# From attention to the output projection of layer 0: a relay of divisors on another queue, a reciprocal in four pieces, and two tiles that take the last heads last

## The chip, the cores and the metric

The kernel is one program for one NeuronCore of a Trainium2 chip. That core has five engines that run at the same time, each with its own list of instructions in a fixed order: TensorE (PE in the profile, with its weight loads as PEld), VectorE (DVE), ScalarE (ACT), GpSimd (POOL) and SyncE (SP). An engine that waits for a semaphore holds back everything that stands behind it in its own list. Data moves by DMAs, which are issued by SP and POOL here and carried out by 16 DMA engines that all queues share.

The metric is device time in microseconds (us) of one execution, and the median over several runs is what counts. Matrix products run in fp32 precision by splitting each operand into a rounded high part and a remainder, so that one product takes three matmuls: high·high, high·low and low·high.

## The reference, cut to what matters

The model has two layers over 1024 positions with a width of 1024. Layer 0 is the one touched here: 12 heads of causal attention with 64 value columns each, beside 4 memory heads, joined and sent through one output projection.

```python
def causal_dense_attention(q, k, v):            # blocks of 128 queries, cut
    sc = einsum('bqhd,bkhd->bhqk', q_blk, k) * scale
    sc = where(mask, sc, NEG)
    p = softmax(sc, axis=-1)
    return einsum('bhqk,bkhd->bqhd', p, v)

for i in range(DEPTH):
    hn = rmsnorm(x, attn_norm_g[i])
    mix, q_cross = mla_mixer(hn, ...) if i % 2 == 0 else swa_mixer(hn, ...)
    cross = memory_cross_attention(q_cross, mem_n, w_mem_kv[i])
    x = x + concatenate([mix, cross], axis=-1) @ w_o[i]
    x = x + squared_relu_mlp(rmsnorm(x, mlp_norm_g[i]), w_up, w_down)
return rmsnorm(x, final_norm_g)
```

The softmax is computed without its division first: the sum of the weights of each query, the divisor, comes out of the same matmul as the weighted values, and the head's output is multiplied by its reciprocal afterwards.

## The kernel before

**Attention.** The loop over `seq` goes through heads 0 to 11, and for each through 12 blocks `(G, k)`: G is one half of the queries (512 columns), k one tile of 128 keys. `scores` (L913) makes the scores of a block in a PSUM tile `pss` by three matmuls; DVE adds the mask on the diagonal part (L921); ACT takes the exponential into `p` (L923). For G = 1 the weights stay whole. For G = 0 they are split (L99 on ACT, L100 on DVE) into `ph` and `pl`. `values` (L943) multiplies them by the values into `pso`, one PSUM tile per head and half. Rows 0 to 63 of `pso` are the head's output, rows 64 to 127 its divisor.

**The heads' divisors.** The outputs of heads 0 to 10 are copied out (L969) and sent by SP to their place in `qn` (L970, called `fa` in the profile for the tiles of heads 8 to 11), and their divisors to a small tile `den` (L973). The heads are divided in groups: 0 to 5, 6 to 9, and 10 alone. For a group, `rc_split` takes the reciprocals of its divisors (L1000), POOL writes them to DRAM (L1001, `rcd`), and POOL reads them back, spread over 64 partitions (L993, `rb`), in two halves of the queries. `rc_mul` (L1010) then multiplies the outputs in place on DVE. For head 10 these are `rb_0_1` (second half) and `rb_0_0` (first half). Head 11 goes another way: `last_o` takes the reciprocal of all 512 columns straight from PSUM (L980) and multiplies (L981), the second half at the end of its values, the first half only inside the output projection.

**The output projection.** `wo_phase` goes over the output columns in two halves. The first half uses weights `wq` loaded earlier (`woq` in the profile); the weights `w1` of the second half are loaded by SP (L689) and split (into `g`) while the first half runs. In the first half the eight row tiles are taken in the order 4, 5, 6, 7, 0, 1, 2, 3, so position p = 0 is tile 4. For each, `load` fetches the tile of x (SP, L1203, two positions ahead); `osp` splits the heads' outputs into high and low parts (`x` in the profile, L99 on ACT and L100 on DVE); `mm3` adds up eight terms in PSUM (`pswo`), 24 matmuls of 512 columns (L108, L109, L110); and DVE adds x (L1278). ACT then takes the sum of squares (L1144). The terms are numbered by pairs of heads: 0 to 3 are heads 0 to 7, 4 is heads 8 and 9, 5 is heads 10 and 11, 6 and 7 are the memory heads. The order is 0, 1, 2, 3, 6, 7, 4, 5. For tiles 4 and 5 the split of terms 4 to 7 goes in two pieces, the memory heads first.

**What sets the order.** The program is recorded in the order of the text, and a scheduler then places the instructions on each engine, mostly by when their operands are due, so the lists of ACT and DVE mix work from attention and projection. DMAs of one engine stand in that engine's list too, so SP issues the loads of x only after what stands ahead of them.

Of the kernel before, what the change touches and what calls it, by code (L numbers as in the profile page):

```python
# [14 lines left out]
ALU = mybir.AluOpType  # L15
# [4 lines left out]
P = 128  # L20
# [35 lines left out]
def trunk(  # L56
# [7 lines left out]
    nc = tc.nc  # L64
    x = x[0]
    out = out[0]
# [518 lines left out]
    halves = [slice(0, 512), slice(512, 1024)]  # L585
# [209 lines left out]
    qn = [(f0, f1)[j // 4][:, j % 4, :] for j in range(6)]  # L795
# [8 lines left out]
    for j in range(6):  # L804
# [4 lines left out]
        ps = ps2(f"pskn{j}")  # L809
# [164 lines left out]

        return mms, then

    def last_o(G, tmp):

        po = po_[(H - 1, G)]
        nc.vector.reciprocal(tmp, po[64:128])  # L980
        nc.vector.tensor_tensor(qn[5][64:128, G * 512 : (G + 1) * 512], po[0:64], tmp, ALU.mult)  # L981


    GRP = [0, 6, 10, 11]
# [4 lines left out]
    def rc_pair(c, j, i):  # L989

        rb = at.tile([P, 512], F32, tag="rb", bufs=4, name=f"rb{c}_{j}_{i}")
        for e in range(min(2, GRP[c + 1] - GRP[c] - 2 * j)):
            nc.gpsimd.dma_start(out=rb[e * 64 : e * 64 + 64, :], in_=rc_d[c][2 * j + e, halves[i]].partition_broadcast(64))  # L993
        return rb

    def rc_split(c):

        n = (GRP[c + 1] - GRP[c]) * NT
        rc = at.tile([48, P], F32, tag="rc", bufs=1, name=f"rc{c}")[:n]
        nc.vector.reciprocal(rc, den[c])  # L1000
        nc.gpsimd.dma_start(out=rc_d[c].rearrange("h (t p) -> (h t) p", p=P), in_=rc)  # L1001
        r_tiles[c] = [(j, i) for j in range((GRP[c + 1] - GRP[c] + 1) // 2) for i in (1, 0)]
        r_tiles[c] = [(j, i, rc_pair(c, j, i)) for j, i in r_tiles[c]]

# [16 lines left out]
    LV, LB = 3, 5  # L1021
    NB = len(blocks)
# [12 lines left out]
    for n in range(len(seq) + LB):  # L1035
        ms, mv, then = [], [], []
        if n < len(seq):
            ms, then_s = scores(*seq[n])
        for lag, late in ((LB, True), (LV, False)):
            if 0 <= n - lag < len(seq):  # L1040
                a, b = values(*seq[n - lag], late)
                mv += a
                then.append(b)

        mix = []
        if ms and mv and P in [width(*seq[n - lag][1:]) for lag in (0, LV, LB)]:
            while ms and mv:
                mix += [ms.pop(0), mv.pop(0)]
        for f in mix + ms:
            f()  # L1050
        if n < len(seq):
            then_s()
        for g, i in ahead.get(n, ()):
            if i < NT:
                row_max(g, i)
            else:
                max_row(g)
        h, j = divmod(n, NB)
        if n < len(seq):
            if h + 1 < H and j == 6:  # L1060
                v_tiles(h + 1)
            if h + 1 < H and j == 8:
                v_full(h + 1)
            if j == (0 if h else 4) and h + 2 < H:
                head_tiles(h + 2)
        for f in mv:
            f()
        for f in then:
            f()
        if n % 2 or n > 11 * NB:  # L1070
            next(muls, None)
        if n >= 9 * NB + 8 and n % 3 == 0:
            wq.step()
        for c in range(3):
            if n == GRP[c + 1] * NB + LB + 1:
                rc_split(c)
            if n == GRP[c + 1] * NB + LB + (8 if c == 2 else 11):
                muls = rc_mul(c)
    for _ in muls:
        pass  # L1080
# [75 lines left out]
    def wo_phase(layer, wq, o, m):  # L1156
# [10 lines left out]
        def o_split(t, parts_=(0, 1), x=None):  # L1167

            r = []
            for i in parts_:  # L1170
                if x is None and layer == 1 and oct_[0] == 0:
                    d = ores.tile([P, 2, 512], F32R, name="ores0")
                    oct_[0] += 1
                elif x is None:
                    d = m.t(f"d{oct_[0] % 3}", F32R)
                    oct_[0] += 1
                else:
                    if x not in ox:
                        ox[x] = m.t(f"x{x % 4}", F32R)
                    d = ox[x][:, 2 * i : 2 * i + 2, :]  # L1180
                oh, ol = k4(d[:, 0, :]), k4(d[:, 1, :])
                src = o[i][:, :, t * P : (t + 1) * P]
                for ks in (slice(2, 4), slice(0, 2)) if i and x in (0, 1) else (slice(0, 4),):
                    split(src[:, ks, :], oh[:, ks, :], ol[:, ks, :])
                r += [(oh[:, k, :], ol[:, k, :]) for k in range(4)]
            return r
# [63 lines left out]
        for half, w in enumerate((wq, w1)):  # L1250
            order = ORD[half]

            def osp(p, parts_):
                t = order[p]
                if half == 1 and t in kept:
                    return kept[t][4 * parts_[0] : 4 * parts_[-1] + 4]
                r = o_split(t, parts_, p if layer == 0 and half == 0 else None)
                if half == 0 and layer == 0 and p in (5, 7):
                    kept[t] = kept.get(t, []) + r
                return r  # L1260

            xs = {0: load(0, half), 1: load(1, half)}
            oo = {0: osp(0, (0, 1))}
            for p in range(NT):
                t = order[p]
                if p + 2 < NT:
                    xs[p + 2] = load(p + 2, half)
                ps = ps1(f"pswo{layer}_{half}_{t}")
                ot = oo.pop(p)
                if p + 1 < NT:  # L1270
                    oo[p + 1] = osp(p + 1, (0,))
                mm3(ps, [(*ot[k], *w.w[k]) for k in (0, 1, 2, 3, 6, 7, 4, 5)])
                if p + 1 < NT:
                    oo[p + 1] += osp(p + 1, (1,))
                if p == 1 and layer == 0 and half == 0:
                    last_o(0, m.t("i39")[0:64, 0, :])
                x_ = xs.pop(p)
                nc.vector.tensor_tensor(x_, ps, x_, ALU.add)  # L1278
                if half == 0:
                    w1.step()  # L1280
                    rst[t] = Rstd()
                    rst[t].half(0, x_, m.t(f"d{3 + p % 2}")[:, 0, :])
                    continue
                for i, v_ in enumerate((xa[t], x_)):
                    nc.gpsimd.dma_start(out=xd[rows_(t), i * 512 : i * 512 + 512], in_=v_)
                norm(p, x_)
                if p:
                    xT_(p - 1)
                if p in (2, 4):
                    m.fill.append(fill_w(layer, m, p // 2 - 1))  # L1290
            if half == 0:
                if layer == 0:
                    new_psum(2)
                for i in range(2):
                    q = m.quad(f"q{i}", F32R)
                    X[i + 1] = [q[:, 0:4, :], q[:, 4:8, :]]
# [781 lines left out]
```

## Time and profile before

| | |
|---|---|
| Median of 3 runs | 2145.2 us (2143.55 to 2147.43) |
| Profiled execution, first to last instruction (span) | 2151.4 us |
| PE busy | 2113.6 us, 98% of the span |
| DVE busy | 1473.3 us, 68% |
| ACT busy | 1106.6 us, 51% |
| POOL busy | 148.9 us, 7% |
| Mean granted TensorE clock | 0.994 |

The profiled execution's own time is given by its span alone: first to last instruction takes 2151.4 us, and what lies around that is not shown. This is 6.2 us, or 0.3%, more than the median of the timed runs.

How to read the rows: a row of the timeline gives the start in us from the span's start, the time from the start of the first to the end of the last instruction in that row, the engine, the line of the kernel, the operation, what it writes and reads, and the shape. Behind it, in brackets, stands how long the engine had been idle before it and what it was waiting for. A row by stretches of time gives, for each engine, the busy time and the number of instructions; then the granted TensorE clock (1.00 is full speed) and the DMA engines' busy share and rate. Matmuls overlap each other, so the time of one is longer than the step from one start to the next.

### The profile page before, as it was taken

The numbers are of one execution on the slowest core, as the hardware profiler recorded it, in microseconds if no ns is written. First come the engines' busy times: TensorE is split into PE (matmuls) and PEld (weight loads), VectorE is DVE, ScalarE is ACT, GpSimd is POOL, SyncE is SP. The second block draws the span as 40 slices with busy tenths as digits, with TensorE's granted clock in tenths as the row PEclk, the third lists the DMA queues.
The fourth block names the chain that finished last, engine by engine and source line by source line (L and its number), as shares of the span: only waits on it lengthen the run. The fifth ranks groups of instructions, "written<-read, shape, count | busy, mean of one in ns | idle before, by whom it ended". The sixth has DMA issues, their size and how long they took to land.

```text
span 2151.4 us, 28963 instructions
## 1 busy us (share of the span) xinstructions
PE 2113.6 (98%) x9830; PEld 1697.7 (79%) x9830; DVE 1473.3 (68%) x2915; ACT 1106.6 (51%) x2406; POOL 148.9 (7%) x251
## 2 busy tenths in 40 slices
PE   7999999989999999999999999999999999999998
PEld 6888766668888788888888878668888888788886
DVE  7767677764987677886557632776987766876665
ACT  6555466655754543444445432866844453444453
POOL 1001001010000000000001121530000000000000
PEclk9999999999999999999999999999999999999999
DMA  6202223333354445954433534132354446954432
GB/s 225 84 1 71 54 67 92 94 114 103 103 174 144 138 162 190 326 179 147 146 115 108 152 79 118 40 128 84 103 181 142 140 149 212 321 167 142 133 119 87
DMA packets 176436, 286.84 MB, mean 133 GB/s; under 512 B 16627, under 2 KB 68448, under 8 KB 176288
## 3 DMA queue, kind: packets, MB, share of 16 engines
q1 hardware_dynamic: 169648, 266.30, 39.1%
q0 software_dynamic: 5328, 16.07, 2.1%
q10 hardware_dynamic: 1312, 2.63, 0.4%
q8 instruction: 77, 1.26, 0.2%
q14 instruction: 71, 0.58, 0.1%
HBM read 183.01 MB, written 76.85 MB: 121 GB/s over the span
## 4 chain that ended last, share of the span: by engine, by line
PE 90%; DVE 4%; DMA 3%; ACT 2%; issue 1%; POOL 0%; SPq 0%; DVEq 0%; ACTq 0%; POOLq 0%
PE psy L1705 5%; PE psy L1707 5%; PE psy L1706 5%; PE psu L1402 5%; PE psu L1404 5%; PE psu L1403 5%; PE psz L1705 4%; PE psz L1707 4%; PE psz L1706 4%; PE psv L1404 4%; PE psv L1403 4%; PE psv L1402 4%; PE pso L943 3%; PE pss L913 3%; PE pswo L110 3%; PE pswo L108 3%
## 5 line engine op out<-in xcount | busy, mean ns | idle before, releaser
L1302 ACT ACTIVATE mr<-mr,gcol 128x256 f32<-128x256 f32 (+1 forms) x160 | 67.6, 477 | 79.4 <-DMA mr<-in_mlp_w_up_dram 70.4
L923 ACT ACTIVATE p<-pss 128x512 f32<-128x512 f32 (+2 forms) x144 | 68.4, 486 | 69.3 <-DVE pss L921 52.4
L1705 PE MATMUL psy<-g 128*128 128x512 f32 x256 | 99.9, 390 | 0.0
L1706 PE MATMUL psy<-g 128*128 128x512 f32 x256 | 99.6, 389 | 0.0
L1707 PE MATMUL psy<-g 128*128 128x512 f32 x256 | 99.4, 390 | 0.0
L99 ACT ACTIVATE g<-i 128x512 fp32r<-128x512 f32 x79 | 49.7, 629 | 93.5 <-PE psz L1706 46.3
L1302 ACT ACTIVATE d<-d,gcol 128x256 f32<-128x256 f32 x128 | 57.6, 500 | 75.2 <-DMA d<-in_mlp_w_up_dram 61.4
L100 DVE TENSOR_TENSOR g<-i,g 128x512 fp32r<-128x512 f32 x79 | 55.5, 703 | 47.8 <-ACT g L99 47.8
L99 ACT ACTIVATE i<-mr 128x512 fp32r<-128x512 f32 x78 | 49.1, 630 | 73.7 <-PE psy L1706 26.1
L943 PE MATMUL pso<-p,vf 128*128 128x512 f32 (+2 forms) x192 | 85.4, 527 | 0.5 <-ACT p L923 0.5
L792 DVE TENSOR_REDUCE m<-psx 128x1 f32<-128x1024 f32 (+7 forms) x96 | 71.9, 752 | 20.0 <-PE psx L791 19.6
L99 ACT ACTIVATE uh<-i 128x512 fp32r<-128x512 f32 x66 | 41.7, 631 | 84.6 <-PE psy L1706 39.3
L100 DVE TENSOR_TENSOR uh<-i,uh 128x512 fp32r<-128x512 f32 x66 | 45.5, 689 | 46.2 <-ACT uh L99 46.2
L1705 PE MATMUL psz<-g 128*128 128x512 f32 x192 | 74.7, 389 | 0.0
L1706 PE MATMUL psz<-g 128*128 128x512 f32 x192 | 74.7, 389 | 0.0
L1707 PE MATMUL psz<-g 128*128 128x512 f32 x192 | 74.7, 389 | 0.0
L100 DVE TENSOR_TENSOR i<-mr,i 128x512 fp32r<-128x512 f32 x78 | 53.5, 686 | 21.5 <-ACT i L99 21.5
L913 PE MATMUL pss<-qh,kh 97*128 97x512 f32 (+2 forms) x144 | 68.0, 474 | 0.0
L1618 DVE TENSOR_TENSOR mqf<-mqq,mqf 128x512 f32<-128x512 f32 x64 | 43.3, 686 | 22.1 <-DMA mqq<-in_mlp_w_down_dram 21.9
L913 PE MATMUL pss<-ql,kh 97*128 97x512 f32 (+2 forms) x144 | 58.2, 404 | 0.0
L1707 PEld LDWEIGHTS psy<-g 128*128 128x128 f32 x256 | 48.1, 188 | 10.1
L1706 PEld LDWEIGHTS psy<-g 128*128 128x128 f32 x256 | 48.1, 188 | 9.9
(655 smaller groups left out, 6890.5 us busy)
## 6 DMA issues: line engine op xcount, KB each, us to landing
i<-hd SPq DMA_DIRECT2D x154, 256.0 KB
hd<-uh SPq DMA_DIRECT2D x76, 256.0 KB
hd<-ul SPq DMA_DIRECT2D x76, 256.0 KB
mr<-in_mlp_w_up_dram SPq DMA_DIRECT2D x36, 512.0 KB
hd<-x SPq DMA_DIRECT2D x72, 256.0 KB
mr<-hd SPq DMA_DIRECT2D x70, 256.0 KB
d<-in_mlp_w_up_dram SPq DMA_DIRECT2D x32, 512.0 KB
mqq<-in_mlp_w_down_dram SPq DMA_DIRECT2D x32, 512.0 KB
```

The source lines that it names most:

```text
L99: nc.scalar.activation(hi, src, AF.Copy)
L100: nc.vector.tensor_tensor(lo, src, f32(hi), ALU.subtract)
L792: nc.vector.reduce_max(m8s[h][:, i : i + 1], ps[:, :n], axis=AX, negate=True)
L913: return lambda: nc.tensor.matmul(o, a, b, skip_group_check=True, **kw)
L943: mms.append(lambda: nc.tensor.matmul(o, a, b, skip_group_check=True, **kw))
L1302: nc.scalar.activation(w[:, k, :], w[:, k, :], AF.Copy, scale=g_mlp[layer][:, k0 + k : k0 + k + 1])
L1402: nc.tensor.matmul(ps, wh[:, k, :], xh[:, k, :], start=p in (1, 2, 5) and k == 0, stop=False, skip_group_check=True)
L1403: nc.tensor.matmul(ps, wh[:, k, :], xl[:, k, :], start=False, stop=False, skip_group_check=True)
L1404: nc.tensor.matmul(ps, wl[:, k, :], xh[:, k, :], start=False, stop=k == 3, skip_group_check=True)
L1705: nc.tensor.matmul(ps, ah[:, j, :], bh, start=p in (1, 5, 2) and k == 0, stop=False, skip_group_check=True)
L1706: nc.tensor.matmul(ps, ah[:, j, :], bl, start=False, stop=False, skip_group_check=True)
L1707: nc.tensor.matmul(ps, al[:, j, :], bh, start=False, stop=k == NP - 1, skip_group_check=True)
```

## The change

The change has five parts, all between the end of attention and the first tiles of the output projection of layer 0.

1. For group 2 (head 10 alone) the write of the reciprocals and the two reads are issued by SP instead of POOL. They stand on SP right after head 10's last output, ahead of the loads of x.
2. The point in the text at which head 10's multiplications begin is two steps later (10 instead of 8).
3. `last_o` works in pieces of 128 columns: four reciprocals and four multiplications, each pair in turn. For the second half of the queries all four come at the end of head 11's values. For the first half one piece comes at each of the positions p = 0 to 3.
4. For tiles 4 and 5 the split of terms 4 to 7 goes in three pieces: memory heads, then heads 8 and 9, then heads 10 and 11.
5. Tiles 4 and 5 first run seven of their eight terms each; term 5 (heads 10 and 11) of tile 4 and of tile 5 follows then, and with it the addition of x and the sum of squares of both.

In the resulting lists SP has three more DMAs, standing between `den<-on` and the first `i<-in_x_dram`, and POOL three fewer. DVE has 14 more instructions: six more reciprocals, six more multiplications, two more splits. ACT has two more splits. PE has the same instructions in another order. Before, PE's list has the first two matmuls each of tiles 4, 5 and 6, then the matmul of `pl_0_1`, then the first two of tile 7, then the last four matmuls of head 11, then the rest of tile 4. After, `pl_0_1` comes first, then the first two matmuls of tiles 4 and 5, the last four matmuls of head 11, the first two of tiles 6 and 7, then the rest. On DVE the order of head 10's multiplications, the splits `pl` and the reciprocals is also different: both multiplications stand ahead of `pl_0_1` and `pl_0_2`, with the mask of the block (0, 2) between them, and the reciprocals of head 11 stand behind all of these. Beyond the first half of the projection, the lists differ by a few exchanged neighbours only.

```diff
-    def last_o(G, tmp):
+    def last_o(G, tmp, js=range(4)):
         po = po_[(H - 1, G)]
-        nc.vector.reciprocal(tmp, po[64:128])
-        nc.vector.tensor_tensor(qn[5][64:128, G * 512 : (G + 1) * 512], po[0:64], tmp, ALU.mult)
+        for j in js:
+            c = slice(j * P, (j + 1) * P)
+            nc.vector.reciprocal(tmp[:, c], po[64:128, c])
+            nc.vector.tensor_tensor(qn[5][64:128, G * 512 + j * P : G * 512 + (j + 1) * P], po[0:64, c], tmp[:, c], ALU.mult)
...
-            nc.gpsimd.dma_start(out=rb[e * 64 : e * 64 + 64, :], in_=rc_d[c][2 * j + e, halves[i]].partition_broadcast(64))
+            (nc.sync if c == 2 else nc.gpsimd).dma_start(out=rb[e * 64 : e * 64 + 64, :], in_=rc_d[c][2 * j + e, halves[i]].partition_broadcast(64))
...
-        nc.gpsimd.dma_start(out=rc_d[c].rearrange("h (t p) -> (h t) p", p=P), in_=rc)
+        (nc.sync if c == 2 else nc.gpsimd).dma_start(out=rc_d[c].rearrange("h (t p) -> (h t) p", p=P), in_=rc)
...
-            if n == GRP[c + 1] * NB + LB + (8 if c == 2 else 11):
+            if n == GRP[c + 1] * NB + LB + (10 if c == 2 else 11):
...
-                for ks in (slice(2, 4), slice(0, 2)) if i and x in (0, 1) else (slice(0, 4),):
+                for ks in (slice(2, 4), slice(0, 1), slice(1, 2)) if i and x in (0, 1) else (slice(0, 4),):
...
-            oo = {0: osp(0, (0, 1))}
+            oo, rest = {0: osp(0, (0, 1))}, []
...
-                mm3(ps, [(*ot[k], *w.w[k]) for k in (0, 1, 2, 3, 6, 7, 4, 5)])
+                terms = [(*ot[k], *w.w[k]) for k in (0, 1, 2, 3, 6, 7, 4, 5)]
+                early = layer == 0 and half == 0 and p < 2
+                mm3(ps, terms[: 7 if early else 8], last=not early)
...
-                if p == 1 and layer == 0 and half == 0:
-                    last_o(0, m.t("i39")[0:64, 0, :])
-                x_ = xs.pop(p)
-                nc.vector.tensor_tensor(x_, ps, x_, ALU.add)
+                if layer == 0 and half == 0 and p < 4:
+                    if p == 0:
+                        od = m.t("i39")[0:64, 0, :]
+                    last_o(0, od, [p])
+                rest.append((p, t, ps, terms[7:] if early else None))
+                if early and p == 0:
+                    continue
+                for q, t, ps, term in rest:
+                    if term:
+                        mm3(ps, term, first=False)
+                    x_ = xs.pop(q)
+                    nc.vector.tensor_tensor(x_, ps, x_, ALU.add)
+                    if half == 0:
+                        w1.step()
+                        rst[t] = Rstd()
+                        rst[t].half(0, x_, m.t(f"d{3 + q % 2}")[:, 0, :])
+                rest = []
                 if half == 0:
-                    w1.step()
-                    rst[t] = Rstd()
-                    rst[t].half(0, x_, m.t(f"d{3 + p % 2}")[:, 0, :])
                     continue
```

## The prediction

> **What bounds the kernel now.** I read the page's summary and its chain of waits first, to see which engine a saving must come from; then stretches of time around the change; then the timelines of PE, DVE, POOL and SP in that stretch, to follow the one long stall back to its cause.
>
> ```profile
> span 2151.4 us, 28963 instructions
> PE 2113.6 (98%) x9830; PEld 1697.7 (79%) x9830; DVE 1473.3 (68%) x2915; ACT 1106.6 (51%) x2406; POOL 148.9 (7%) x251
> PE 90%; DVE 4%; DMA 3%; ACT 2%; issue 1%; POOL 0%; SPq 0%; DVEq 0%; ACTq 0%; POOLq 0%
> ```
>
> PE is 90% of the chain that ends last. A microsecond in which PE is idle or slow is paid in full; one saved on another engine counts only if PE waited for it.
>
> ```profile
> 453.00:456.00 3.00, 2.77 (x11) 1.38 (x9) 0.00 (x0) 2.62 (x6) 0.88 (x2) 1.00 0.79 262
> 456.00:461.50 5.50, 0.01 (x1) 0.01 (x1) 4.52 (x4) 0.00 (x0) 0.00 (x0) 0.75 0.02 4
> 461.50:464.50 3.00, 2.55 (x7) 1.57 (x8) 2.94 (x8) 1.93 (x6) 0.00 (x0) 0.50 0.00 0
> 464.50:469.00 4.50, 4.50 (x13) 3.53 (x13) 4.47 (x8) 3.13 (x5) 0.00 (x0) 0.50 0.17 62
> 469.00:477.10 8.10, 8.10 (x36) 6.53 (x35) 6.16 (x8) 2.52 (x6) 0.57 (x1) 1.00 0.09 33
> 477.10:509.50 32.40, 32.40 (x140) 26.07 (x139) 16.00 (x21) 19.59 (x46) 3.24 (x6) 1.00 0.46 146
> ```
>
> After the length stand PE, PEld, DVE, ACT and POOL; the third number from the end is the granted clock. PE does nothing from 456 to 461.5, and then works at a clock of 0.50 until 469. So the stall is paid twice.
>
> ```profile
> 455.49 0.40 PE L109 MATMUL pswo<-woq,x 128*128 128x512 f32 x1
> 461.49 0.69 PE L943 MATMUL pso<-pl,vh 128*128 128x384 f32 x1 [5.60 <-DVE pl L100]
> 464.53 0.73 PE L110 MATMUL pswo<-woq,x 128*128 128x512 f32 x1
> 476.66 0.63 PE L110 MATMUL pswo<-woq,x 128*128 128x512 f32 x2
> 481.79 0.63 PE L110 MATMUL pswo<-woq,x 128*128 128x512 f32 x2
> ```
>
> PE waits for `pl_0_1`, a split of 0.5 us on DVE. The rest of tile 4 begins at 464.53. The pair at 476.66 is tile 5's last matmul and tile 6's first one of the rest, the latter 0.23 later, at 476.89.
>
> ```profile
> 445.34 0.94 DVE L1000 RECIPROCAL rc<-den 8x128 f32<-8x128 f32 x1
> 451.13 0.60 DVE L921 TENSOR_TENSOR pss<-pss,dmaskT 128x128 f32<-128x128 f32 x2
> 456.95 0.68 DVE L1010 TENSOR_TENSOR fa<-rb,fa 64x512 f32<-64x512 f32 x1 [5.22 <-DMA rb<-rcd]
> 457.66 3.36 DVE L980 RECIPROCAL rq<-pso 64x512 f32<-64x512 f32 x1
> 460.94 0.82 DVE L100 TENSOR_TENSOR pl<-p,ph 128x384 fp32r<-128x384 f32 x2
> 461.79 0.69 DVE L981 TENSOR_TENSOR fa<-pso,rq 64x512 f32<-64x512 f32 x1
> 463.32 0.68 DVE L100 TENSOR_TENSOR x<-qn,x 128x512 fp32r<-128x512 f32 x1
> 463.93 0.28 DVE L100 TENSOR_TENSOR pl<-p,ph 128x128 fp32r<-128x128 f32 x1
> 464.13 0.74 DVE L100 TENSOR_TENSOR x<-fa,x 128x256 fp32r<-128x256 f32 x2
> ```
>
> DVE itself waits: `fa<-rb` stands ahead of the splits and needs the divisors of head 10. Behind it come a reciprocal of 3.36 us and only then `pl`.
>
> ```profile
> 432.44 0.50 POOL L1001 DMA_DIRECT2D rcd<-rc  x1 [62.18 <-DVE pl L100]
> 434.37 4.11 POOL L993 DMA_DIRECT2D rb<-rcd  x8 [1.43 <-DMA rcd<-rc]
> 446.57 0.53 POOL L1001 DMA_DIRECT2D rcd<-rc  x1 [8.09 <-DVE rc L1000]
> 452.83 1.05 POOL L993 DMA_DIRECT2D rb<-rcd  x2 [5.73 <-DMA rcd<-rc]
> 443.50 0.61 SPq L973 DMA_DIRECT2D den<-on  x1
> 444.17 8.91 SPq L1203 DMA_DIRECT2D i<-in_x_dram  x10
> ```
>
> The relay through DRAM starts at 446.57, when SP has already issued several of x's loads of 256 KB.
>
> ```profile
> rcd<-rc POOLq DMA_DIRECT2D x1, 16.0 KB, 1.6
> rcd<-rc POOLq DMA_DIRECT2D x1, 4.0 KB, 6.0
> DMA to landing us min/median/max: 2.8/2.9/4.1
> L1000 DVE RECIPROCAL rc<-den x3: 930/934/940, 360.4 to 445.3; 48x128 f32<-48x128 f32 x1, 32x128 f32<-32x128 f32 x1, 8x128 f32<-8x128 f32 x1
> ```
>
> The last number of the first two rows is the time from issue to landing: 1.6 us for the group before, 6.0 for the smaller write of head 10. The third row is that of `rb` (L993). From the end of the reciprocal, 445.34 + 0.94 = 446.28, to `fa<-rb` at 456.95 the relay takes 10.67 us.
>
> **The change part by part.**
>
> *The relay on SP.* POOL started 0.29 after the reciprocal's end (446.57 against 446.28); I keep this for SP. No row gives the landing of such a write from SP. The nearest is `den<-on`, issued at 443.50 and used by DVE at 445.34, so at most 1.84; the write from POOL without x's loads took 434.37 − 432.44 = 1.93 until the next issue. I take 1.93, as this row holds issue, landing and wake-up. For the read I take the shortest of L993's row, 2.8, since no load of x is in flight then. So `rb_0_1` lands at 446.28 + 0.29 + 1.93 + 2.8 = 451.3. DVE is then just done with the first of the two masks (451.13 plus half of 0.60, 451.4), so an earlier landing gains nothing; that is the one end. The other is 10.67 us again, landing at 456.9. `rb_0_0` is issued 0.6 later and lands while DVE works on the first.
>
> A rule speaks against this part. The Trainium skill, "DMA: Bandwidth & Descriptors", section "Issuing engines are not separate DMA queues", says that transfers of all issuing engines share the same 16 DMA engines and interleave, so that another issuing engine saves issue time only. By that alone the relay stays at 10.67 us, and the sum is that of rival B. The two write rows differ by 4.4 us on the same queue, so what stands beside the transfer matters; the order ahead of x removes this whichever engine issues.
>
> *The order on DVE.* From 451.4 on: `fa<-rb_0_1` 0.61 (the step from 463.32 to 463.93), mask 0.2, `fa<-rb_0_0` 0.61, `pl_0_1` and `pl_0_2` 0.82 (the row at 460.94), then for tile 4 three reciprocals of 128 columns with two multiplications, a mask and `pl_0_3`, then the split `x<-qn`. A reciprocal of 128 columns took 0.93 to 0.94 whatever its rows (L1000), a 128-column step 0.20 (463.93 to 464.13). So 0.61 + 0.2 + 0.61 + 0.82 + 3 × 0.93 + 4 × 0.20 + 0.61 = 6.4, and `x<-qn` ends at 457.8. PE follows about 0.1 later, at 457.9, with the rest of tile 4, against 464.53: **6.6 us**.
>
> The four pieces cost 4 × 0.93 = 3.7 instead of 3.36 per half, but the fourth and the later multiplications lie behind `x<-qn`: PE needs `x<-fa` of tile 4 only ten matmuls later, at 457.9 + 10 × 0.233 = 460.2, and DVE has it after 0.93 + 0.2 + 0.4, at 459.4.
>
> *PE until then.* `pl_0_1` comes at 453.7, so PE's work goes on: it has six matmuls of 512 columns, the rest of head 11 and two more, with waits of some tenths for ACT. I count about 1.2 us of idle time in pieces from 453.5 to 457.9. The new wait is that mask (0, 2), hence `ph_0_2`, stands behind `rb_0_1`. It is due on PE at 453.4, and is done at 453.1: 0.3 us of cover. Each us that the relay is later than that stops PE for as long.
>
> *The clock.* Tiles 4 and 5 have 44 matmuls left. Before, they took 464.53 to 476.89, 12.36 us. A tile's 22 take 481.79 − 476.66 = 5.13 at full clock, so 10.26. If the clock stays at 1.00, **2.1 us** more are saved. Rows for both outcomes:
>
> ```profile
> 35.52:38.94 3.42, 1.46 (x6) 0.86 (x5) 3.13 (x11) 1.78 (x4) 0.00 (x0) 1.00 0.00 0
> 38.94:45.76 6.82, 5.54 (x24) 5.17 (x25) 5.74 (x25) 3.52 (x7) 0.00 (x0) 0.50 0.46 155
> 144.75:148.16 3.41, 2.49 (x19) 2.31 (x18) 3.11 (x10) 2.50 (x7) 1.43 (x4) 1.00 0.01 2
> 148.16:151.58 3.42, 3.42 (x25) 3.38 (x24) 2.02 (x4) 3.41 (x12) 0.81 (x1) 1.00 0.00 0
> ```
>
> With 1.46 of 3.42 us busy (43%) the clock fell to 0.50 afterwards; with 2.49 of 3.41 (73%) it did not. I expect about 3.2 of 4.4 busy, 73%.
>
> *The last heads last.* PE does the same 44 matmuls, so it costs nothing there. Tile 4's addition comes after tile 5, and its split buffer is free for the fifth tile 5.1 us later. Cover: tiles 6 and 7, 2 × 5.13 = 10.3 us of PE work, against some 2 us for the splits. Without it, PE would wait those 2 us. The six extra reciprocals and multiplications and two splits on DVE, and two splits on ACT, lie in stretches where these have slack (16.00 and 19.59 busy of 32.40).
>
> *SP and POOL.* SP issues x's first load after both reads, at 446.57 + 1.93 + 1.2 = 449.7 instead of 444.17. It is used at 457.9 + 10.3 = 468.2, so 18 us are left; ten loads took 8.91 to issue before. Everything behind them on SP (the weights of the second half) waits for DVE's and PE's work, which is earlier now. On POOL nothing stood behind the two reads before the first store of x. Cost: nothing. The later start in the text of head 10's multiplications has only the effect of the order above.
>
> *Sum.* 6.6 + 2.1 = 8.7 us. The profiled span goes from 2151.4 to 2142.7. It is 6.2 above the median of 2145.2; I carry the difference over: **2136.5 us**.
>
> **The rivals.**
>
> *A: the clock falls all the same.* If PE's idle pieces meet in one stretch, or the relay is 1 to 2 us later, the share comes down towards 43%. Before, 0.50 lasted from about 458.8 to 469, some 10.2 us (0.75 is the mean of 456 to 461.5); in the rows above, 6.8. With PE at work throughout this costs 3.4 to 5.1: 2139.9 to 2141.6. For it: the margin is thin. Against it: the row at 73%. The Trainium skill, "TensorE: Matmul & The Clock Gate", section "What's actually happening", has the clock halved after one idle window of about 3.4 us; by that rule pieces of idle time of a few tenths leave it alone. The rows above agree at 73%, while at 43% the window was not idle and the clock fell.
>
> *B: the relay takes 10.67 us on SP as well.* Then everything from 451.4 moves by 5.5: PE stops at 453.4, the rest of tile 4 starts at 463.4, and the clock falls as before (about 2.6 lost), so tile 6 begins at 463.4 + 10.3 + 2.6 = 476.3 instead of 476.9: 2144.6, no change. Against it: 1.6 against 6.0.
>
> *C: slower.* The place is DVE's wait for `rb_0_1`: the mask, both `pl` and with them PE now stand behind it, and the six early matmuls too, which before ran during the wait. Past a landing at 457.5 each us costs one; 0.2% slower needs 461.8, a relay of 15.5 us: 2149.5 or more. No row shows one over 10.67.
>
> *D: the gain is given back* in the second half of the projection, if its weights or x come late: 2143 to 2145. Against it: PE is busy 32.40 of 32.40 us up to 509.5.
>
> **How the numbers follow.** Forecast 72%, A 13%, B 6%, D 5%, C 4%. The likeliest one's own range is 2134.3 to 2138.7: the runs lie up to 2.2 from their median, and a read of 4.1 instead of 2.8 gives 1.3. With A it reaches to 2141.6. About 0.2%, 4.3 us, is what a measurement can tell from no change, so faster means below 2140.9: the forecast, half of A and some of D, 83%. Within it lie the rest of A, B and D, 12%; slower 5%, C and what I don't see.
>
> **What would show it.** `rcd` on SP lands in about 2 us and `fa<-rb` starts near 451.4 with next to no wait; PE's 5.60 at `pl` is gone, no idle piece is over 1 us between 453 and 458; tile 4's rest starts near 458; the clock reads 1.00 from 440 to 509; the first addition of x comes near 468 and waits for PE, not for x. The prediction is wrong if `fa<-rb` waits past 453, if the clock reads 0.50 anywhere there, or if an idle piece as long as the gain turns up after 468.

## The result, and the profile after

The changed kernel takes **2139.24 us** (median of 9 runs, 2137.54 to 2141.73), beside 2145.2 us of the kernel before (median of 9 runs, 2142.95 to 2149.52): a ratio of 0.9969, with a 95% interval of 0.996 to 0.9978, or 6.0 us less. Forecast was 2136.5, with 2134.3 to 2141.6 as the range; the likeliest case had 2134.3 to 2138.7 of it, so the measured time lies 0.5 us beyond that part, in what rival A added.

The profiled execution has a span of 2137.4 us, and its own run took 2139.06. From the page of the changed kernel, the same three lines as shown of before:

```profile
span 2137.4 us, 28982 instructions
PE 2107.2 (99%) x9830; PEld 1695.1 (79%) x9830; DVE 1475.4 (69%) x2929; ACT 1106.3 (52%) x2408; POOL 147.3 (7%) x248
PE 92%; DVE 3%; DMA 2%; ACT 2%; issue 1%; SPq 0%; DVEq 0%; ACTq 0%
```

Two spans can't simply be subtracted: 14.0 us lie between these two, and not all of them come from the change. Head 10's reciprocal, which is ahead of all that was edited, ends at 442.06 + 0.94 = 443.00 now and ended at 446.28 before, so 3.3 of the 14.0 are there by then. I therefore count everything from that end, and call a time so counted R+. The first matmul of the projection's second half comes at R+55.06, and came at R+63.28: **8.2 us** around the change. The last 2.5 us are small pieces further back; part of them, near 700 to 880 us, also differs by up to 2 us between two executions of the changed kernel.

The stretch around the change, in the view by stretches of time (length; busy time and number on PE, PEld, DVE, ACT, POOL; granted clock; DMA share and rate):

```profile
449.00:452.00 3.00, 2.71 (x15) 1.87 (x14) 2.91 (x6) 2.70 (x8) 0.00 (x0) 1.00 0.88 278
452.00:455.30 3.30, 2.22 (x10) 1.25 (x9) 3.18 (x7) 2.30 (x8) 0.00 (x0) 1.00 1.02 381
455.30:465.54 10.24, 10.24 (x46) 8.31 (x46) 9.93 (x20) 5.35 (x8) 0.00 (x0) 1.00 0.09 35
465.54:473.80 8.26, 8.26 (x37) 6.72 (x36) 8.07 (x13) 5.74 (x13) 1.66 (x3) 1.00 0.36 134
473.80:506.20 32.40, 32.40 (x142) 26.40 (x141) 14.13 (x20) 18.67 (x44) 3.23 (x6) 1.00 0.41 133
```

The clock is 1.00 in every row. There is no row in which PE does nothing, and DVE is nearly full until 473.8; in the kernel before it stood still for 5.22 us ahead of `fa<-rb`. PE's own rows:

```profile
451.55 0.50 PE L108 MATMUL pswo<-woq,x 128*128 128x512 f32 x1 [0.29 <-ACT x L99]
452.98 0.33 PE L943 MATMUL pso<-ph,vh 128*128 128x128 f32 x1 [0.71 <-ACT ph L99]
453.21 0.43 PE L943 MATMUL pso<-pl,vh 128*128 128x256 f32 x2
454.01 0.50 PE L108 MATMUL pswo<-woq,x 128*128 128x512 f32 x1 [0.37 <-ACT x L99]
455.31 0.40 PE L110 MATMUL pswo<-woq,x 128*128 128x512 f32 x1
465.30 0.62 PE L110 MATMUL pswo<-woq,x 128*128 128x512 f32 x2
```

The wait of 5.60 us for `pl` is gone, and three waits of 0.29, 0.71 and 0.37 us are left. The rest of tile 4 starts at 455.31 (R+12.3, before R+18.25). The pair at 465.30 is the last matmul of tile 5 and the first of tile 6's rest, at 465.53 (R+22.5, before R+30.6). DVE and SP:

```profile
442.06 0.94 DVE L1002 RECIPROCAL rc<-den 8x128 f32<-8x128 f32 x1
447.86 0.29 DVE L921 TENSOR_TENSOR pss<-pss,dmaskT 128x128 f32<-128x128 f32 x1
448.06 0.67 DVE L1012 TENSOR_TENSOR fa<-rb,fa 64x512 f32<-64x512 f32 x1
449.46 0.95 DVE L100 TENSOR_TENSOR pl<-p,ph 128x384 fp32r<-128x384 f32 x2
450.44 0.96 DVE L982 RECIPROCAL rq<-pso 64x128 f32<-64x128 f32 x1
451.43 0.30 DVE L921 TENSOR_TENSOR pss<-pss,dmaskT 128x128 f32<-128x128 f32 x1
451.76 0.28 DVE L983 TENSOR_TENSOR fa<-pso,rq 64x128 f32<-64x128 f32 x1
452.08 0.96 DVE L982 RECIPROCAL rq<-pso 64x128 f32<-64x128 f32 x1
453.60 0.96 DVE L982 RECIPROCAL rq<-pso 64x128 f32<-64x128 f32 x1
454.48 0.62 DVE L100 TENSOR_TENSOR x<-qn,x 128x512 fp32r<-128x512 f32 x1
456.33 0.36 DVE L100 TENSOR_TENSOR x<-fa,x 128x256 fp32r<-128x256 f32 x1
464.93 1.16 DVE L100 TENSOR_TENSOR g<-wor,g 128x1024 fp32r<-128x1024 f32 x1
466.12 1.29 DVE L1290 TENSOR_TENSOR i<-pswo,i 128x512 f32<-128x512 f32 x2
```

```profile
443.03 0.32 SPq L1003 DMA_DIRECT2D rcd<-rc  x1
444.41 1.13 SPq L995 DMA_DIRECT2D rb<-rcd  x2
445.59 8.14 SPq L1205 DMA_DIRECT2D i<-in_x_dram  x11
```

SP issues the write at R+0.03 and the first read at R+1.40. DVE comes to `fa<-rb` at R+5.05, straight from the mask and without a wait, and ends `x<-qn` at 455.10, R+12.1. PE follows 0.2 later, when it has done the four early matmuls of tiles 6 and 7 (454.01 to 455.31).

From the start of `fa<-rb` to the end of `x<-qn` DVE takes 12.10 − 5.05 = 7.05 us. In the kernel before it is the same: 456.95 to 463.32 + 0.68 = 464.00, also 7.05. So DVE's new order and its pieces, taken together, don't bring the split nearer; what is saved up to there is the relay's 10.67 − 5.05 = 5.62.

### The profile page after: what moved, and what is told of

Its sections match the earlier page's. It is cut to its first block, busy times and chain, and to the rows that moved or that the text cites. A ratio compares the mean times of both kernels' runs of the same rounds, so it can differ in the third digit from the quotient of the medians.

```text
span 2137.4 us, 28982 instructions
## 1 busy us (share of the span) xinstructions
PE 2107.2 (99%) x9830; PEld 1695.1 (79%) x9830; DVE 1475.4 (69%) x2929; ACT 1106.3 (52%) x2408; POOL 147.3 (7%) x248
## 4 chain that ended last, share of the span: by engine, by line
PE 92%; DVE 3%; DMA 2%; ACT 2%; issue 1%; SPq 0%; DVEq 0%; ACTq 0%
PE psu L1416 5%; PE psy L1721 5%; PE psy L1719 5%; PE psu L1418 5%; PE psu L1417 5%; PE psy L1720 5%; PE psz L1721 4%; PE psz L1720 4%; PE psz L1719 4%; PE psv L1418 4%; PE psv L1416 4%; PE psv L1417 4%; PE pso L943 4%; PE pss L913 3%; PE pswo L108 3%; PE pswo L110 3%
```

## The experiments

Each kernel ran beside the kernel before on the same chip, and its ratio is to that. Positions are counted from R as above, so that differences at the start of an execution drop out.

### The size of what can be told apart: `e1_same`

The kernel before with a constant written as `10 + 1`: the same instructions.

> The kernel before, unchanged in every instruction. It shows how much two equal kernels differ, and how the clock falls after the stall in another execution. I measure from the end of head 10's reciprocal (L1000) to the first matmul of tile 6's rest; before this is 476.89 - 446.28 = 30.6 us, after it is 465.53 - 443.00 = 22.5. If the stall always costs the same, 30.6 again. If the clock's windows lie elsewhere, the time at a clock of 0.50 is 6.8 instead of 10.2 us and the distance up to 1.7 us shorter. Time: 2145 within 0.1%.

Measured: 2147.91 beside 2148.03, ratio 1.0002 (0.9994 to 1.0011). The value is in the profile: a second execution of the kernel before. By stretches of time, the stall up to the rest of tile 4, and from there to tile 6's:

```profile
449.08:459.36 10.28, 4.57 (x14) 2.28 (x13) 7.48 (x11) 3.79 (x10) 0.00 (x0) 0.75 0.23 69
459.36:470.39 11.03, 11.03 (x46) 8.94 (x46) 10.59 (x14) 5.61 (x10) 0.57 (x1) 0.93 0.14 49
```

The stall is nearly the same (tile 4's rest at R+17.8 instead of R+18.25, after a relay of 10.2 instead of 10.67), but the clock reads 0.50 for 6.8 us, not 10.2, and the 44 matmuls take 11.03, not 12.36. The first matmul of the second half comes at R+61.34, 1.9 earlier than in the first execution and 6.3 later than in the changed kernel. So the stall hardly differs from execution to execution, and the fall of the clock behind it does.

### The relay alone, and the rest alone: `e2_relay`, `e3_rest`

The first is the kernel before with parts 1 and 2 of the change, the second the changed kernel with its relay back on POOL.

```diff
 e2_relay, to before
-            nc.gpsimd.dma_start(out=rb[...
+            (nc.sync if c == 2 else nc.gpsimd).dma_start(out=rb[...
-        nc.gpsimd.dma_start(out=rc_d[c]...
+        (nc.sync if c == 2 else nc.gpsimd).dma_start(out=rc_d[c]...
-            ... (8 if c == 2 else 11)
+            ... (10 if c == 2 else 11)
 e3_rest, to after
-            (nc.sync if c == 2 else nc.gpsimd).dma_start(out=rb[...
+            nc.gpsimd.dma_start(out=rb[...
-        (nc.sync if c == 2 else nc.gpsimd).dma_start(out=rc_d[c]...
+        nc.gpsimd.dma_start(out=rc_d[c]...
```

> The kernel before with parts 1 and 2 alone: head 10's divisors by SyncE ahead of x's loads, the later start in the text; whole reciprocals and the old order of terms stay. Theory (the relay's wait is the whole stall): fa<-rb starts 5.1 us after the reciprocal's end, DVE then has 2.2 us of masks and splits, 3.3 us of reciprocal, 1.5 us of mask, multiplication and x<-qn, so tile 4's rest starts 12.3 us after it, as in the kernel after (455.31 - 443.00 = 12.3), the distance is 22.5 to 23 and the whole gain is there, 6 us in the time. Rival (the pieces and the late terms are needed, since the whole reciprocal stops PE for over 3 us and the clock falls): distance 25 to 27 with a clock of 0.50, and a third to two thirds of the gain.

> The kernel after with part 1 undone: the relay is on POOL beside x's loads again; pieces, three-way split, late terms and the later start in the text stay. Theory (the relay's wait is the whole stall): the relay takes 10 to 11 us again, tile 4's rest starts 17 to 18 us after the reciprocal's end, the clock falls to 0.50, the distance is 29 to 31, and the time is that of before within 2 us. Rival (the pieces and the late terms bring the gain): distance under 27, time 2139 to 2142.

Measured: the relay alone 2143.11, ratio 0.9981 (0.9971 to 0.999). The rest alone 2149.81, ratio 1.0013 (1.0005 to 1.0022), a little slower. The relay alone, the same two stretches:

```profile
450.82:455.94 5.12, 3.23 (x13) 1.63 (x11) 5.03 (x5) 3.42 (x10) 0.00 (x0) 1.00 0.92 331
455.94:467.91 11.97, 11.97 (x46) 9.67 (x46) 11.06 (x15) 6.52 (x12) 0.58 (x1) 0.86 0.14 50
```

Tile 4's rest starts at R+12.62, only 0.3 later than with the whole change, so that parts 1 and 2 are nearly all of what the stall loses. But the 44 matmuls take 11.97 instead of 10.23: the clock reads 0.50 for 3.4 us of them. In the kernel with the rest alone DVE waits for the reads as before:

```profile
452.22 0.68 DVE L1012 TENSOR_TENSOR fa<-rb,fa 64x512 f32<-64x512 f32 x1 [4.75 <-DMA rb<-rcd]
453.81 0.82 DVE L100 TENSOR_TENSOR pl<-p,ph 128x384 fp32r<-128x384 f32 x2
459.92 0.69 DVE L100 TENSOR_TENSOR x<-qn,x 128x512 fp32r<-128x512 f32 x1
```

The scheduler orders DVE's list anew here: both masks stand ahead of `fa<-rb`, and the second `fa<-rb` behind the reciprocals. `pl` comes sooner after `fa<-rb` than in the kernel before (1.6 us, not 4.0), but `x<-qn` ends 8.4 us after it, not 7.05, as four reciprocals and four multiplications stand between. Tile 4's rest starts at R+18.65, 0.4 to 0.9 later than in the two executions of the kernel before: with a late relay the rest of the change costs, and the pieces are what stands between.

### The queue or the order: `e4_poolx`

The kernel before, relay on POOL as it was, but with layer 0's loads of x issued by POOL behind it.

```diff
-            nc.sync.dma_start(out=dst, in_=m.x_src[...
+            (nc.gpsimd if layer == 0 else nc.sync).dma_start(out=dst, in_=m.x_src[...
```

> The kernel before with the relay left on POOL, but x's loads of layer 0 (L1203) issued by POOL too, where they stand behind the relay's three DMAs. PE, DVE and ACT keep their lists. Theory (it is the order ahead of x's loads that counts, not the engine that issues): the write lands in about 1.6 us, the read in 2.8, fa<-rb starts 5 us after the reciprocal's end instead of 10.7, PE's idle 5.60 us at pl falls to under 1, the clock stays at 1.00, the distance is 22.5 to 24, the time 2138 to 2141. Rival (SyncE's queue is what is faster): the relay takes 10 us or more, the time stays at 2145.

Measured: 2142.86, ratio 0.9976 (0.9967 to 0.9986). POOL's own DMAs, and the two stretches:

```profile
442.26 0.53 POOL L1001 DMA_DIRECT2D rcd<-rc  x1 [8.12 <-DVE rc L1000]
444.14 1.05 POOL L993 DMA_DIRECT2D rb<-rcd  x2 [1.35 <-DMA rcd<-rc]
445.17 5.43 POOL L1203 DMA_DIRECT2D i<-in_x_dram  x10
```

```profile
449.47:454.81 5.34, 3.86 (x14) 1.70 (x13) 5.28 (x9) 3.72 (x10) 1.06 (x2) 0.99 0.92 332
454.81:466.66 11.85, 11.85 (x45) 9.51 (x46) 10.68 (x14) 5.70 (x10) 1.08 (x2) 0.86 0.15 52
```

From the write to the next issue POOL now needs 1.88 us, against 6.26 before; `fa<-rb` starts at R+5.36 against 5.05 on SP, and tile 4's rest at R+12.84. The write lands 1.6 us after its issue, and took 6.0 in the kernel before. So it was the loads of x beside the relay that made it late, and not the queue. This agrees with the Trainium skill, "DMA: Bandwidth & Descriptors", section "Issuing engines are not separate DMA queues", in that another engine buys nothing but issue time. What that rule would have made of this change (rival B) did not come, as the change also reorders.

### The other parts, one by one: `e5_after`, `e6_whole`, `e7_noterm`, `e8_split_first`

The changed kernel; the same with one whole reciprocal for the second half of the queries; the same without the last heads last (part 5); and one that goes further: the four pieces of the second half move from the end of attention into the projection, so that tile 4's split `x<-qn` comes ahead of them.

```diff
 e6_whole, to after
-        for j in js:
-            c = slice(j * P, (j + 1) * P)
+        for c, j in [(slice(0, 512), 0)] if len(js) == 4 else [(slice(j * P, (j + 1) * P), j) for j in js]:
 e7_noterm, to after
-                early = layer == 0 and half == 0 and p < 2
+                early = False
 e8_split_first, to after
-                if G:
-                    last_o(G, at.tile([64, 512], F32, tag="on", bufs=2, name="rq1"))
...
                 for ks in (slice(2, 4), slice(0, 1), slice(1, 2)) if i and x in (0, 1) else (slice(0, 4),):
+                    if i and x is not None and x < 4 and ks.stop != (4 if x < 2 else 0) and ks.stop != 1:
+                        if x == 0:
+                            od1.append(m.t("i30")[0:64, 0, :])
+                        last_o(1, od1[0], [x])
```

> The kernel after, unchanged in every instruction. From the end of head 10's reciprocal to tile 6's rest its profile had 22.5 us and no fall of the clock, the kernel before 30.6 and 28.8 in two executions. Theory (the forecast's sum with the clock as the term that varies): 22.5 again if the clock stays at 1.00, up to 24.2 if one window of 3.4 us falls to 0.50; the stall's part, tile 4's rest 12.3 us after the reciprocal's end, is the same to 0.1. Time 0.996 to 0.998 of before. Rival (part of the gain is given back after the projection): the distance is 22.5 and yet the time is under 5 us below before, with new idle pieces of PE after tile 6.

> The kernel after with whole reciprocals for the second half of the queries (3.36 us in one, one multiplication of 512 columns); all else stays. Theory (the pieces only keep PE fed while it waits): tile 4's rest starts 12 to 12.7 us after the reciprocal's end as in the kernel after, but PE has one idle piece of 1.5 us or more in place of three under 0.8, the clock can fall as with the relay alone, so the distance is 22.5 to 24.7 and the time 0 to 2 us above the kernel after. Rival (the whole reciprocal delays tile 4): tile 4's rest 14 us or later, time 2 us or more above.

> The kernel after with part 5 undone: tiles 4 and 5 run all their eight terms in one go. Theory (the last heads of tile 4 are split 14.5 us after the reciprocal's end, and PE asks for them 4.4 us after the start of tile 4's rest, at 16.7, so the late terms hide nothing): no wait of PE for x<-fa, distance 22.5 (24.2 if the clock falls), time that of the kernel after within 1 us. Rival (the late terms are needed): PE waits 1 us or more at term 5 of tile 4 and the distance grows by as much.

> A version of the kernel after in which the second half's four reciprocals and multiplications stand inside the projection too, each just before the split that needs it, so that DVE splits tile 4's first heads (x<-qn) before any of them. Theory (what is left of PE's wait is DVE's reciprocals ahead of that split): DVE ends x<-qn about 8.3 us after the reciprocal's end instead of 12.1, tile 4's rest starts near 8.7 instead of 12.3, the distance is 19.5 to 20.5, and the time 2 to 3 us below the kernel after (four early matmuls of tiles 6 and 7, 0.9 us, come later instead). Rival (another wait takes its place, on ph of block (0, 3) or on the last heads): tile 4's rest before 10 but the distance at 22 or more, time as the kernel after.

| | time | ratio, 95% | `x<-qn` ends | tile 4's rest | tile 6's rest | second half starts | clock at 0.50 |
|---|---|---|---|---|---|---|---|
| `e5_after` | 2139.05 | 0.9964 (0.9952 to 0.9977) | R+12.09 | R+12.30 | R+22.52 | R+55.05 | none |
| `e6_whole` | 2143.01 | 0.9981 (0.9972 to 0.999) | R+12.56 | R+12.62 | R+24.53 | R+57.20 | 3.4 us |
| `e7_noterm` | 2140.45 | 0.9973 (0.9963 to 0.9984) | R+12.10 | R+12.29 | R+22.52 | R+55.05 | none |
| `e8_split_first` | 2137.94 | 0.9962 (0.9948 to 0.9975) | R+8.20 | R+9.11 | R+19.38 | R+54.26 | none |

With the whole reciprocal the split comes 0.5 later, the clock falls once, and the second half comes 2.15 us later; both together are what the pieces bring. Without part 5 every position in the table is the same to 0.01 us, so that part hides nothing here; the difference in time is within the intervals.

Of what the last one was to bring, half came or less. Tile 4's rest starts 3.2 earlier, and the last matmul of the first half is at R+53.08 against R+54.82, 1.7 earlier. But then this row stands in PE's timeline:

```profile
497.39 0.50 PE L108 MATMUL pswo<-g,d 128*128 128x512 f32 x1 [0.78 <-DVE i L1292]
```

The first matmul of the second half waits for the addition on DVE that empties a tile of PSUM. The work moved into the projection comes back as a wait of 0.78, 0.8 us of gain are left, and the time can't be told from that of the changed kernel.

### What the clock is worth by itself: `e9_fill`, `e10_whole`, `e11_after`, `e12_fill6`

The pieces of the reciprocal change two things at once, the split's time and PE's idle time. To part them, useless matmuls fill idle time in the kernel with the whole reciprocal (`e6_whole`). In the first they write to an unused tile early on; in the last PE repeats tile 6's first matmul, which starts its sum anew each time. The other two are `e6_whole` and the changed kernel again, on the chip of the first; the last ran on another chip.

```diff
 e9_fill, to e6_whole
+        if n == len(seq) + 1:
+            fl = psx("fill")
+            for e in range(4):
+                nc.tensor.matmul(fl[:, 0:512], bufs_[(H - 1) % 3][2][:, 0:P], bufs_[(H - 1) % 3][0][:, 0:512], start=True, stop=True, skip_group_check=True)
 e12_fill6, to e6_whole
+                if layer == 0 and half == 0 and p == 2:
+                    for e in range(4):
+                        nc.tensor.matmul(ps, terms[0][0], terms[0][2], start=True, stop=False, skip_group_check=True)
```

> The kernel with the whole reciprocal for the second half of the queries, plus four matmuls of 512 columns that write to an unused PSUM tile and are read by nobody. They stand on PE ahead of the matmul of pl_0_0, so that 4 x 0.233 = 0.93 us of work goes into the idle pieces of 0.28, 0.29 and 1.18 us that follow; nothing else moves. Theory: the pieces of 128 columns in the reciprocal are worth the clock and little else. Then the fillers do the same without them: the busy share of the window rises from 0.57 to about 0.84, the clock reads 1.00 all through, x<-qn still ends 12.56 after head 10's reciprocal, but the first matmul of the second half comes at 55.2 instead of 57.20, and the time is 2 to 4 us below that kernel without the fillers, about as the changed kernel. Rival: the pieces help because the operands come earlier, or the clock falls because of the stall whatever PE does in it. Then the fillers bring nothing or cost up to 0.93: the clock reads 0.50 for 3.4 us or more, the first matmul of the second half is at 57.2 to 58.1, and the time is level with that kernel or up to 1 us above it.

> The same without the fillers, beside it on the same chip: the clock falls again, for 3.4 us or for 6.8 us; the first matmul of the second half is at 57.2 with 3.4, near 58.9 with 6.8. Time 2 to 5 us above the changed kernel. If the clock stays at 1.00 in this execution, the share of 0.57 is not below a fixed limit and the fall is a matter of the single execution.

> The changed kernel beside both: the clock reads 1.00 through the stretch, the first matmul of the second half at 55.05, ratio to the kernel before 0.9964 as in the call before. If the clock falls here, part of the gain comes and goes with the execution.

> The kernel with the whole reciprocal for the second half of the queries, in which PE repeats the first matmul of tile 6 four times (the first of a sum starts it anew, so that the repeats are useless work). They stand between the pair of tile 5 and that of tile 6, where their operands are there at 9.6 after head 10's reciprocal, ahead of the idle piece of 1.18 us in which PE waits for ACT's p. ACT and DVE keep their order, so the piece shrinks by 4 x 0.233 = 0.93. Theory: the pieces in the reciprocal are worth the clock and little else. Then the busy share of the window rises from 0.55-0.57 to about 0.82, the clock reads 1.00 all through, x<-qn still ends 12.56 after the reciprocal and the rest of tile 4 begins at 12.6, but that of tile 6 comes at 22.9 instead of 24.53-24.66 and the first matmul of the second half at 55.3 instead of 57.2-57.3; ratio to the kernel before 0.9964 as the changed kernel (0.9955 to 0.997). Rival: the clock falls after this stall whatever PE does in it. Then tile 6's rest and the second half come at 24.6 and 57.3 as without the fillers, the clock reads 0.50 for 3.4 us, and the ratio is 0.998.

Measured: `e9_fill` 2144.08, ratio 0.9984 (0.9975 to 0.9993); `e10_whole` 2141.85, 0.9977 (0.9967 to 0.9986); `e11_after` 2140.3, 0.9964 (0.9952 to 0.9976); `e12_fill6` 2142.25, 0.9977 (0.9967 to 0.9987).

The repeats of two kernels came as before: with the whole reciprocal the clock falls for 3.4 us and the second half is at R+57.33; in the changed kernel it doesn't, and it is at R+55.05.

`e9_fill` missed its aim. With the filling the pair of tile 7 waits for DVE's multiplication, and no longer for ACT's `p`, and it waits longer:

```profile
455.32 0.47 PE L108 MATMUL pswo<-woq,x 128*128 128x512 f32 x1 [1.68 <-DVE fa L982]
```

The idle pieces of 0.28, 0.29 and 1.18, 1.75 in all, became one of 1.68, hardly less, and the clock fell as before. It says nothing of the question. In `e12_fill6` the wait for ACT's `p` stays, and shrinks:

```profile
449.82 1.19 PE L1277 MATMUL pswo<-woq,x 128*128 128x512 f32 x4 [0.29 <-ACT x L99]
451.74 0.50 PE L108 MATMUL pswo<-woq,x 128*128 128x512 f32 x1 [0.27 <-ACT p L923]
```

```profile
447.75:452.87 5.12, 4.15 (x18) 2.38 (x16) 5.03 (x5) 3.82 (x12) 0.00 (x0) 1.00 0.90 336
452.87:463.32 10.45, 10.45 (x46) 8.54 (x47) 10.19 (x20) 4.89 (x8) 0.00 (x0) 1.00 0.10 32
```

Tile 4's rest starts at R+12.62, as without the repeats, so nothing arrives earlier. But the clock stays at 1.00, and the second half is at R+55.60 (forecast 55.3) instead of 57.20 to 57.33: 1.6 us won by useless work. So in this execution it was enough to keep PE busy for the clock to stay, with DVE and ACT as late as before. The timed runs don't confirm this: 0.9977 is the ratio without the repeats too. Their intervals of 0.001 to each side (2.1 us) are wider than the 1.6 in question. The mean granted clock that is reported with every run reads 0.998 in 8 of its 12 runs and 0.996 in 4, so it may be that the clock still fell in some. That stays open.

## Why the prediction was right, and what was mis-sized

**The relay** was right in place and in size. Landing was forecast in time for the end of the first mask, 5.1 after R; `fa<-rb` starts at R+5.05 and doesn't wait. The write took 1.38 from issue to the read's issue, not 1.93, and SP took it up 0.03 after the reciprocal's end, not 0.29. This 0.8 gained nothing, as the prediction said an earlier landing would, since DVE is busy until then. The reason, the order ahead of x, is shown by `e4_poolx`. Rival B, a relay as long on SP as on POOL, is out.

**DVE's order** was mis-sized by 0.7: from `fa<-rb` to the end of `x<-qn` it takes 7.05, forecast 6.4. I charged 0.20 for a step of 128 columns, taken from one that starts while its neighbour still runs. Here the four such steps (a mask, two multiplications and `pl_0_3`, as 451.43 to 451.76 and 451.76 to 452.08) take 0.32 to 0.33 each, 0.5 more in all, and the two `pl` take 0.98 (449.46 to 450.44) instead of 0.82. That each step waits for the result ahead of it isn't the whole reason: the mask at 451.43 and the reciprocal at 452.08 need nothing of the instruction ahead, and still start 0.03 behind its end. What sets this step stays open. So tile 4's rest begins at R+12.30, forecast 11.6: the term of 6.6 measures 5.95 against the profile of before, and 5.5 against `e1_same`, whose relay took 10.2 instead of 10.67.

**PE until then**: three waits of 0.29, 0.71 and 0.37, 1.37 in all, forecast about 1.2 in pieces; from 450.51 to 455.31, where tile 4's rest begins, PE is busy for 3.43 of 4.80 us, 71%, forecast 73%. None is over 1 us.

**The clock** stayed at 1.00 in all three profiles of the changed kernel, so rival A is out for them, but with little room. Leaving out the start and the end of each profile, the stretches at 0.50 last 3.41, 6.83 or 10.24 us, so I count in windows of 3.41 us, laid out from the clock's own changes in the same execution. The window that holds the stall's last part ends at R+12.1 to R+12.8. In `e2_relay`, `e4_poolx`, `e6_whole`, `e9_fill` and `e10_whole`, with 51% to 60% of it busy, the clock fell each time; in the changed kernel it has 68% to 69%.

The size of the term, 2.1, was read from one execution, and there it holds: 12.36 against 10.23 for the 44 matmuls. In `e1_same` it is 0.8. The fall begins at the same place in both, R+12.50 and R+12.57, and ends one window later in the first, where PE was busy for 0.87 of the second slow window; in `e1_same` it was 1.00. The Trainium skill, "TensorE: Matmul & The Clock Gate", section "What's actually happening", calls the window free-running, and puts the varying number of slow matmuls at a kernel's start down to where it lies. Here the lengths vary too, 6.8 and 10.2, but with windows that lie alike to 0.07 us. That the busy share of the window decides isn't shown: elsewhere the clock rose behind 0.83 (`e7_noterm`, from 38.3 us) and 0.87 (the changed kernel, from 55.7), and stayed low behind 0.95 (`e3_rest`, from 454.3).

How often each length comes can be estimated from the mean granted clock of all runs: 0.9956 over 105 runs of the kernel before (`e1_same` among them) and 0.9976 over 22 of the changed kernel. The difference of 0.0020 (standard error 0.0002), times 2142 us and divided by the 0.50 that is lost, is 8.6 us less at half clock. This lies between the 6.8 and the 10.2 of the two profiles; between their prices of 0.8 and 2.1 it stands for 1.5 us, if the clock's other falls in the program are alike.

**The sum** is then 5.5 to 5.95 and 1.5, 7.0 to 7.4 us, where 8.7 was forecast. Counted directly, the second half comes 6.3 us earlier than in `e1_same` and 8.2 earlier than in the profile of before. The three comparisons give 0.9969, 0.9964 and 0.9964, times 2147 us 6.7 to 7.7. That fits. So the step that went too far is the sum made against one execution: its stall was longer by 0.4 and its fall of the clock by 3.4 us than those of another, and DVE's chain was forecast too short by 0.7. That the time still lies in the stated range is in part luck: it lies beyond the 2138.7 of the likeliest case, in the stretch added for rival A, which none of the profiles of the changed kernel shows. (With the 0.9964 of the other two comparisons it would be 2137.5, inside.)

**The span** was forecast at 2142.7 and is 2137.4. The profile of before was 6.2 above the median; that of after is 1.8 below. Every run that lists both has a time 1.7 us above its span (2139.06 and 2137.4 here), so the profiled execution of before took some 2153.1, 3.6 more than the longest of the nine timed beside the changed kernel, and that of after is near its median. Carrying the 6.2 over was right for the time, and wrong for the span; it also means that the stall and the clock's fall were read from an execution longer than usual.

**The last heads last, the additions, SP and POOL** cost nothing, as said: no wait between 455.3 and 506.2, and x comes in time. One point fell: the first addition was to wait for PE. It comes at R+23.1, forecast 21.9, and waits for DVE itself, behind a split of 1.16 us for the second half's weights (464.93). PE's next use of that buffer is far away, so it cost nothing. That this part wins nothing (`e7_noterm`) was not in the prediction, and neither was what the pieces are worth alone.

**Rivals C and D**: a relay long enough for C, with the changed kernel's DVE list, came in no run. `e3_rest` doesn't test it, as its list is another one, with the masks ahead of `fa<-rb`; it shows that the rest of the change costs 0.4 to 0.9 with a late relay. Nothing was given back in the second half: its last matmul comes at R+103.85, against R+112.04 before, 8.2 us as at its start. So D is out. Parts 2 and 4 weren't tried by themselves. In `e4_poolx`, which has neither, tile 4's rest is 0.54 later than with all parts.

## What to carry to other kernels

A small transfer on the critical path belongs ahead of large loads that aren't urgent; which engine issues it mattered little here (tile 4's rest at R+12.84 from POOL, R+12.62 from SP). Take the step between two instructions from a row in which the same kinds follow each other: the 0.20 between two splits was 0.32 between a multiplication and a reciprocal. And where an idle stretch lets the clock fall, take that price from more than one execution, by counting from a mark just ahead of the edit.

## What the runs showed of the hardware

- The clock fell to 0.50 behind windows of about 3.4 us in which PE was busy for 0.00 to 0.60 of the time around this place (eight profiles), and not behind 0.62, 0.68, 0.69, 0.84 and 0.93. The Trainium skill, "TensorE: Matmul & The Clock Gate", section "What's actually happening", speaks of an idle window; here a window more than half busy was enough. It is no fixed limit: near 36 and 50 us windows of 0.41 to 0.60 busy passed without a fall (0.41 in `e5_after`, 0.53 in `e10_whole`, 0.60 in `e12_fill6`).
- Much of the spread between runs of one kernel goes with the mean granted clock: over the 105 runs of the kernel before, the span is 1.5 us shorter for each 0.001 more (correlation −0.72).
- SP took up a DMA 0.03 us after the instruction it waited for had ended (the changed kernel, `e2_relay`), POOL 0.29 (the kernel before, `e4_poolx`).
- A reciprocal of 128 columns took 0.94 us on 8 partitions and 0.96 on 64 (the changed kernel).
- A write of 4 KB took 6.0 us from issue to landing on POOL's queue with loads of 256 KB issued just ahead by SP (the kernel before), and 1.6 with these loads behind it (`e4_poolx`).
